# Sums of the second product's weights tied behind the blocks of the first: a hybrid decoder block on one core

## The chip, the cores and the metric

The kernel runs on one core of a Trainium2 chip. The core has five engines that work side by side, each through its own queue, in the order in which the instructions were put there: TensorE (PE in the profile; PEld is its weight load), VectorE (DVE), ScalarE (ACT), GpSimd (POOL) and SyncE (SP). DMAs are issued from the queues of SP and ACT. The metric is the device time of one execution in microseconds (us), lower is better. A profiled execution gives a trace with a start, a duration and, where an engine stood idle, a releaser for each instruction.

## The reference

The program is one decoder layer on a sequence of 1024 rows with 1024 channels: a token-selecting attention and a causal convolution side by side, merged by gates, then a dense feed-forward part, all in float32. The change lies in the feed-forward part:

```python
h = modulate(rmsnorm(x, norm_ffn_g[l]), sh_f, sc_f)
a, b = jnp.split(h @ w_ffn_in[l], 2, axis=-1)              # (1024 x 1024) @ (1024 x 5632)
x = x + g_f[:, None, :] * ((jax.nn.silu(a) * b) @ w_ffn_out[l])   # (1024 x 2816) @ (2816 x 1024)
return rmsnorm(x, norm_final_g)
```

## The kernel before

Both products are done in Strassen-Winograd form: instead of eight products of quarter matrices, seven, with sums and differences of quarters on both sides. Each float32 operand is split into a high part (rounded by ACT, L1190) and a low part (the rest, by VectorE or GpSimd, L1191), and one product of quarters is high x high, high x low and low x high: `prod`, L1211 to L1213, 12 matmuls of 128x512. The splits of the weight side go through eight places of a tile `sa`; the activation side (`h2a`, and `T`, which holds B22 and T1 to T4) is split once (`split_t`, L1336 and L1337).

The first product runs over 22 blocks n, one for each 128 columns of w_ffn_in in both halves. A block loads two pieces of w_ffn_in into the tile `ws` (two buffers, `stage_w`, SP), adds them up on VectorE (`s_sums`, L1241 to L1244), and evacuates its PSUM banks. For the first seven blocks (n < NPRE = 7) the two products on h2a come early (`do_m1`, `do_m2`, L1226, L1233), while T is still being made from the last rows of the normed input, and the five others later (`do_apart`). From block 7 on (`do_sums`) two further products are added into the same bank `u`: this is the steady part. The last instruction of a steady block is L1289, `e0 = u * e0` on VectorE, which also frees the bank of u. After each odd block `g_sums` makes the sums of the activation side of the second product from two blocks and stores seven pieces (L1305, seven DMAs on ACT's queue).

The second product needs sums of the quarters of w_ffn_out as well: T1 to T4. `w_sums(j)`, j = 0 to 10, makes them for one j. It loads two row blocks of w_ffn_out (512 KB each) into two buffers of the tile `wt` (L1312, SP), does four VectorE sums in place (L1315 to L1318), and stores the four results to DRAM (L1320, four DMAs on ACT's queue), from where the second product reads them. The tile wt has two buffers, so the loads of set j+1 wait for the stores of set j. In the program text two sets stand behind each odd block from block 7 on, but the text does not set the order. A scheduler places each instruction on its engine by a simulated timeline; what depends on nothing can be placed far ahead. `after(ins, prev)` ties an instruction behind another in the order only, without a semaphore.

## Time and profile before

| | |
|---|---|
| runs | 1620.33 us median of 3 (1613.86 to 1622.17) |
| profiled execution | 1617.23 us, its span 1615.5 us |
| TensorE busy | 1496.8 us, 93% of the span |
| VectorE busy | 1184.9 us, 73% |
| ScalarE busy | 692.0 us, 43% |
| GpSimd busy | 550.6 us, 34% |
| mean granted TensorE clock | 0.971 |
| the chain that ended last | TensorE 53%, VectorE 27%, DMA 8% |

The shares are means over stages with different limits. The stage of the change begins at 935 us, when TensorE leaves the output projection, and its blocks from number 7 on run from about 1114 us. The granted clock is given as a share of 2.4 GHz.

### The profile page before, as it was taken

The numbers are of one execution on the slowest core, as the hardware profiler recorded it, in microseconds if no ns is written. First come the engines' busy times: TensorE is split into PE (matmuls) and PEld (weight loads), VectorE is DVE, ScalarE is ACT, GpSimd is POOL, SyncE is SP. The second block draws the span as 40 slices with busy tenths as digits, with TensorE's granted clock in tenths as the row PEclk, the third lists the DMA queues.
The fourth block names the chain that finished last, engine by engine and source line by source line (L and its number), as shares of the span: only waits on it lengthen the run. The fifth ranks groups of instructions, "written<-read, shape, count | busy, mean of one in ns | idle before, by whom it ended". The sixth has DMA issues, their size and how long they took to land.

```text
span 1615.5 us, 19899 instructions
## 1 busy us (share of the span) xinstructions
PE 1496.8 (93%) x6880; PEld 1203.3 (74%) x6880; DVE 1184.9 (73%) x2100; ACT 692.0 (43%) x1243; POOL 550.6 (34%) x411
## 2 busy tenths in 40 slices
PE   5998999999769999989989997998999999999996
PEld 3776777787648887768767886776888888888875
DVE  5698768999985657756695589998666666555688
ACT  4301456767135555755333344123333333344344
POOL 0232215798939894101440255320000000004172
PEclk9999999999969999989999998999999999999998
DMA  9335332232212222345763435776333334766682
GB/s 348 111 121 186 122 113 56 62 104 86 80 44 66 59 59 79 99 163 163 249 218 120 143 131 176 248 244 230 124 105 98 98 98 138 241 195 193 196 274 106
DMA packets 193597, 232.15 MB, mean 144 GB/s; under 512 B 12152, under 2 KB 126040, under 8 KB 193496
## 3 DMA queue, kind: packets, MB, share of 16 engines
q1 hardware_dynamic: 164416, 174.39, 34.4%
q10 hardware_dynamic: 29080, 56.48, 9.2%
q8 instruction: 54, 0.88, 0.2%
q14 instruction: 47, 0.39, 0.1%
HBM read 167.12 MB, written 59.51 MB: 140 GB/s over the span
## 4 chain that ended last, share of the span: by engine, by line
PE 53%; DVE 27%; DMA 8%; issue 4%; ACT 3%; POOL 3%; SPq 0%; ACTq 0%; DVEq 0%; POOLq 0%
DVE cy L527 5%; PE pj L326 4%; DVE jk L714 4%; PE pj L327 4%; PE pj L328 4%; PE qk L567 3%; PE qk L1211 3%; PE qk L1212 3%; PE qk L1213 3%; PE qk L1115 2%; PE pj L1211 2%; PE pj L1212 2%; PE pj L1213 2%; PE pj L1115 2%; PE pv L870 1%
## 5 line engine op out<-in xcount | busy, mean ns | idle before, releaser
L326 PE MATMUL pj<-hT,wh 128*128 128x512 f32 (+1 forms) x592 | 242.7, 410 | 15.0 <-DVE z L494 5.5
L327 PE MATMUL pj<-hT,wh 128*128 128x512 f32 (+1 forms) x592 | 234.9, 397 | 0.0
L328 PE MATMUL pj<-hT,wl 128*128 128x512 f32 (+1 forms) x592 | 234.5, 396 | 0.0
L125 POOL TENSOR_TENSOR wl<-ws,wh 128x1024 fp32r<-128x1024 f32 (+2 forms) x49 | 127.0, 2593 | 266.9 <-ACT wh L124 241.4
L1476 POOL TENSOR_TENSOR cb<-cb 128x512 f32<-128x512 f32 x8 | 18.1, 2268 | 395.4 <-DVE cb L1495 395.4
L326 PEld LDWEIGHTS pj<-hT,wh 128*128 128x128 f32 (+1 forms) x592 | 112.8, 191 | 42.5 <-DVE z L494 5.7
L1419 DVE TENSOR_TENSOR sa<-sab,sa 128x1024 fp32r<-128x1024 f32 x66 | 94.5, 1438 | 64.5 <-ACT sa L1418 57.8
L328 PEld LDWEIGHTS pj<-hT,wl 128*128 128x128 f32 (+1 forms) x592 | 112.3, 190 | 26.2 <-issue 0.8
L327 PEld LDWEIGHTS pj<-hT,wh 128*128 128x128 f32 (+1 forms) x592 | 112.8, 191 | 19.5 <-issue 0.6
L1418 ACT ACTIVATE sa<-sab 128x1024 fp32r<-128x1024 f32 x66 | 69.9, 1060 | 101.9 <-PE pt L1425 31.0
L1190 ACT ACTIVATE sa<-s 128x512 fp32r<-128x512 f32 x88 | 55.0, 631 | 127.3 <-DMA tT<-wt 26.0
L714 DVE TENSOR_SCALAR_CACHE_REDUCE jk<-M,F 128x640 f32<-128x640 f32 (+4 forms) x136 | 104.4, 821 | 1.7 <-POOL M L675 0.4
L842 ACT ACTIVATE P<-qk,mins 128x384 f32<-128x384 f32 (+4 forms) x96 | 55.2, 578 | 99.0 <-DVE mins L837 94.6
L527 DVE SCALAR_TENSOR_TENSOR cy<-z,dwc,cy 128x511 f32<-128x511 f32 (+29 forms) x120 | 87.9, 801 | 0.1
L724 ACT ACTIVATE jka<-M,F 128x896 f32<-128x896 f32 x64 | 69.7, 1092 | 34.5 <-DVE F L735 31.9
L857 DVE TENSOR_TENSOR PT<-pt,PT 128x512 fp32r<-128x512 f32 (+1 forms) x80 | 50.6, 634 | 38.8 <-ACT PT L856 38.2
L124 ACT ACTIVATE wh<-ws 128x1024 fp32r<-128x1024 f32 (+2 forms) x51 | 48.3, 948 | 69.1 <-PE pj L327 45.1
L466 POOL TENSOR_TENSOR gy<-gy,pr 128x512 f32<-128x512 f32 (+30 forms) x60 | 76.5, 1274 | 2.0
L466 POOL TENSOR_TENSOR cy<-cy,pr 128x512 f32<-128x512 f32 (+30 forms) x60 | 74.1, 1235 | 4.7
L1211 PE MATMUL qk<-T,sa 128*128 128x512 f32 x176 | 69.7, 397 | 6.4 <-ACT E L1226 6.4
L1190 ACT ACTIVATE sa<-ws 128x512 fp32r<-128x512 f32 x66 | 40.9, 629 | 80.4 <-PE qk L1212 26.8
L1191 DVE TENSOR_TENSOR sa<-s,sa 128x512 fp32r<-128x512 f32 x74 | 54.2, 748 | 23.2 <-ACT sa L1190 23.2
(462 smaller groups left out, 4091.5 us busy)
## 6 DMA issues: line engine op xcount, KB each, us to landing
ws<-in_w_ffn_in SPq DMA_DIRECT2D x51, 512.0 KB, 3.8
ws<-in_w_in SPq DMA_DIRECT2D x40, 512.0 KB, 3.6
mst<-in_w_ada SPq DMA_DIRECT2D x32, 512.0 KB, 3.9
wt<-in_w_ffn_out SPq DMA_DIRECT2D x22, 512.0 KB, 3.5
tT<-wt ACTq DMA_DIRECT2D x44, 256.0 KB, 2.4
sab<-gS SPq DMA_DIRECT2D x44, 256.0 KB
sab<-tT SPq DMA_DIRECT2D x44, 256.0 KB, 3.0
sab<-gA SPq DMA_DIRECT2D x33, 256.0 KB, 3.8
```

The source lines that it names most:

```text
L125: (eng or lo_eng[0]).tensor_tensor(view(lo), view(st), view(hi).bitcast(F32), op=ALU.subtract)
L326: nc.tensor.matmul(p_[:m], wh[:, k, :], hh, start=(k == 0), stop=False)
L327: nc.tensor.matmul(p_[:m], wh[:, k, :], hl, start=False, stop=False)
L328: nc.tensor.matmul(p_[:m], wl[:, k, :], hh, start=False, stop=(k == nk - 1))
L466: g_.tensor_tensor(y[:, a:hi], y[:, a:hi], pr[:, : hi - a], op=ALU.add)
L527: v_.scalar_tensor_tensor(y[:, a:hi], z[:, a - sft : hi - sft], tap(cc, CW - 1 - sft), y[:, a:hi], op0=ALU.mult, op1=ALU.add)
L714: v_.tensor_scalar(jk[:, : (tb + 1) * P], M[tb], thr[:, i : i + 1], 0.0, op0=op, op1=ALU.add, accum_out=cnt[:, i : i + 1])
L1190: s_.activation(d[:, 0, :], src, AF.Copy)
L1211: nc.tensor.matmul(bank, a[:, 0, ks], bh, start=(first and k == 0), stop=False, skip_group_check=True)
L1212: nc.tensor.matmul(bank, a[:, 0, ks], bl, start=False, stop=False, skip_group_check=True)
L1213: nc.tensor.matmul(bank, a[:, 1, ks], bh, start=False, stop=(k == 3), skip_group_check=True)
L1419: eng.tensor_tensor(lo, st, hi.bitcast(F32), op=ALU.subtract)
```

## The change

`do_sums` returns its last instruction (L1289), and `w_sums` ties its first two sums behind that instruction of the block after which it is called. The loads, the other two sums and the stores are as before; these follow from the first two by their data.

```diff
         prod(u, r["A22"], T4, False)
-        v_.tensor_tensor(e0, u, e0, op=ALU.mult)
+        return v_.tensor_tensor(e0, u, e0, op=ALU.mult)
...
-    def w_sums(j):
+    def w_sums(j, prev):
 
         rows_ = []
         for f in (j, j + NH2):
...
         (b11, b12), (b21, b22) = rows_
-        v_.tensor_tensor(b11, b12, b11, op=ALU.subtract)
-        v_.tensor_tensor(b12, b22, b12, op=ALU.subtract)
+        for ins in (v_.tensor_tensor(b11, b12, b11, op=ALU.subtract), v_.tensor_tensor(b12, b22, b12, op=ALU.subtract)):
+            after(ins, prev)
         v_.tensor_tensor(b22, b22, b11, op=ALU.subtract)
         v_.tensor_tensor(b21, b21, b22, op=ALU.subtract)
...
             do_m2(n)
-            do_sums(n)
+            last_e = do_sums(n)
         if n % 2:
             g_sums(n)
             for _ in range(0 if n < NPRE else 2):
                 if todo_w:
-                    w_sums(todo_w.popleft())
+                    w_sums(todo_w.popleft(), last_e)
```

What this does to the order of the instructions is seen at three places. In the rows, a name with its number is one tile; both of the first two sums read L1315 in the new kernel, since they stand in one line.

The first place is VectorE's queue where the last quarter of T is made: h_1590 is the last piece of the normed input, L1158 the end of its preparation, and L1337 with T_8668 the low half of T1. The rows before:

```order
L1243 TENSOR_TENSOR s_1629_8737<-ws_8732,ws_8734 128x512
L1318 TENSOR_TENSOR wt_9598<-wt_9598 128x512
L1356 SCALAR_TENSOR_TENSOR h_1581_8218<-h_1581_8218,h2a 128x512
L1158 TENSOR_TENSOR h_1590_8273<-h_1590_8273,h2a 128x512
L1315 TENSOR_TENSOR wt_9869<-wt_9869 128x512
L1233 TENSOR_TENSOR E_8530<-pv_8545,E_8530 128x512
L1242 TENSOR_TENSOR s_1628_8736<-s_1628_8736,ws_8732 128x512
L1191 TENSOR_TENSOR sa_8294<-s_1628_8736,sa_8294 128x512
L1233 TENSOR_TENSOR E_8566<-qk_8581,E_8566 128x512
L1350 TENSOR_TENSOR h_1590_8273<-h_1590_8273 128x512
L1233 TENSOR_TENSOR E_8602<-pj_8617,E_8602 128x512
L1337 TENSOR_TENSOR T_8668<-h_1590_8273,T_8668 128x4x128
```

And the same place in the new kernel, up to the fourth sum of the block, L1244:

```order
L1356 SCALAR_TENSOR_TENSOR h_1581_8218<-h_1581_8218,h2a 128x512
L1158 TENSOR_TENSOR h_1590_8273<-h_1590_8273,h2a 128x512
L1241 TENSOR_TENSOR s_1628_8736<-ws_8734 128x512
L1243 TENSOR_TENSOR s_1629_8737<-ws_8732,ws_8734 128x512
L1350 TENSOR_TENSOR h_1590_8273<-h_1590_8273 128x512
L1233 TENSOR_TENSOR E_8530<-pv_8545,E_8530 128x512
L1242 TENSOR_TENSOR s_1628_8736<-s_1628_8736,ws_8732 128x512
L1337 TENSOR_TENSOR T_8668<-h_1590_8273,T_8668 128x4x128
L1233 TENSOR_TENSOR E_8566<-qk_8581,E_8566 128x512
L1191 TENSOR_TENSOR sa_8294<-s_1628_8736,sa_8294 128x512
L1244 TENSOR_TENSOR s_1629_8737<-ws_8732,s_1628_8736 128x512
```

The sums on wt are gone from here, L1158 stands ahead of L1241 and L1243, and L1337 on T_8668 stands ahead of two evacuations (L1233) and a split (L1191) that came before it.

The second place is VectorE's queue in steady block 10, in the new kernel: wt_9881 and wt_9883 are the second set behind block 9, L1280 and L1285 evacuate block 10, L1191 on ws_10020 is the split of A22 of block 11, and L1241 begins the sums of block 12:

```order
L1191 TENSOR_TENSOR sa_8294<-s_1748_10023,sa_8294 128x512
L1315 TENSOR_TENSOR wt_9881<-wt_9881 128x512
L1191 TENSOR_TENSOR sa_8294<-ws_10034,sa_8294 128x512
L1280 TENSOR_TENSOR G_9932<-pv_9933,G_9932 128x512
L1285 TENSOR_TENSOR G_9932<-qk_9989,G_9932 128x512
L1315 TENSOR_TENSOR wt_9881<-wt_9883,wt_9881 128x512
L1191 TENSOR_TENSOR sa_8294<-ws_10020,sa_8294 128x512
L1317 TENSOR_TENSOR wt_9883<-wt_9883,wt_9881 128x512
L1287 TENSOR_TENSOR G_9932<-G_9932 128x512
L1318 TENSOR_TENSOR wt_9883<-wt_9883 128x512
L1233 TENSOR_TENSOR E_9974<-qk_10042,E_9974 128x512
L1241 TENSOR_TENSOR s_1761_10182<-ws_10180 128x512
```

Before, the same rows stood there without the four on wt. The two rows that follow are L1243 and then L1289 of block 10; the first set (wt_9869 and wt_9871) stands right behind L1289 of block 9, its L1316 six rows behind it, with other rows between.

The third place is SP's queue, which issues the loads of ws for the blocks (L1196) and those of wt (L1312). The steady part of it before:

```order
L1196 DMA ws_9909<-in_w_ffn_in 128x8x128
L1196 DMA ws_10020<-in_w_ffn_in 128x8x128
L1196 DMA ws_10034<-in_w_ffn_in 128x8x128
L1196 DMA ws_10180<-in_w_ffn_in 128x8x128
L1196 DMA ws_10194<-in_w_ffn_in 128x8x128
```

And in the new kernel:

```order
L1196 DMA ws_9909<-in_w_ffn_in 128x8x128
L1196 DMA ws_10020<-in_w_ffn_in 128x8x128
L1196 DMA ws_10034<-in_w_ffn_in 128x8x128
L1312 DMA wt_9881<-in_w_ffn_out 128x1024
L1312 DMA wt_9883<-in_w_ffn_out 128x1024
L1196 DMA ws_10180<-in_w_ffn_in 128x8x128
L1312 DMA wt_10154<-in_w_ffn_out 128x1024
L1312 DMA wt_10156<-in_w_ffn_out 128x1024
L1196 DMA ws_10194<-in_w_ffn_in 128x8x128
```

Before, all loads of wt stood ahead of the steady part, between the loads of ws for the first blocks; now 20 of the 22 stand between the loads of the steady blocks. The stores (L1320) moved on ACT's queue in the same way.

## Rows read from the trace of the kernel before

**Rows 1.** Windows of the first product: busy us (instructions) per engine, granted clock, DMA.

```profile
core 0: us, PE busy (x) PEld busy (x) DVE busy (x) ACT busy (x) POOL busy (x), PEclk, DMA share, GB/s
935.44:1000.00 64.56, 55.66 (x233) 44.05 (x232) 62.11 (x79) 32.39 (x57) 42.06 (x23) 0.92 0.48 161
1000.00:1098.96 98.96, 92.31 (x392) 73.66 (x390) 92.81 (x127) 23.02 (x38) 24.40 (x15) 0.98 0.74 247
1098.96:1121.00 22.04, 15.65 (x58) 12.65 (x59) 17.83 (x30) 7.54 (x14) 0.00 (x0) 0.85 0.71 244
1121.00:1340.00 219.00, 219.00 (x958) 179.39 (x957) 140.34 (x223) 82.35 (x139) 0.00 (x0) 1.00 0.33 106
```

**Rows 2.** Waits of TensorE from 860 us on: total us, times, longest.

```profile
PE qk L1211 <- ACT E L1226: 6.4, 1, 6.4
...
PE pj L1211 <- ACT T L1336: 3.9, 1, 3.9
PE pj L1211 <- ACT sa L1190: 2.6, 1, 2.6
...
PE pj L1211 <- DVE G L1257: 2.0, 1, 2.0
PE pj L1213 <- POOL sa L1191: 1.2, 2, 0.7
PE pt L1211 <- DVE G L1260: 0.9, 1, 0.9
```

**Rows 3.** Windows of the instructions on tile wt alone: VectorE busy (instructions).

```profile
935.44:985.00 49.56, 10.13 (x9) 0.92 0.44 149
1000.00:1100.00 100.00, 25.89 (x27) 0.98 0.74 248
```

**Rows 4.** Timeline of VectorE, first window: start, duration, instruction, idle before it.

```profile
938.74 1.23 DVE L1316 TENSOR_TENSOR wt<-wt,wt 128x512 f32<-128x512 f32 x1 [2.03 <-DMA wt<-in_w_ffn_out]
...
983.11 0.67 DVE L1337 TENSOR_TENSOR T<-h,T 128x512 fp32r<-128x512 f32 x1
```

**Rows 5.** Timeline of TensorE, its first matmul on T.

```profile
978.62 0.79 PE L1211 MATMUL pt<-T,sa 128*128 128x512 f32 x1 [5.02 <-ACT T L1336]
```

**Rows 6.** Timeline of GpSimd and VectorE over one early block.

```profile
1045.81 1.75 POOL L1191 TENSOR_TENSOR sa<-ws,sa 128x512 fp32r<-128x512 f32 x1
...
1052.82 0.69 DVE L1241 TENSOR_TENSOR s<-ws 128x512 f32<-128x512 f32 x1 [0.53 <-DMA ws<-in_w_ffn_in]
...
1056.66 1.29 POOL L1191 TENSOR_TENSOR sa<-s,sa 128x512 fp32r<-128x512 f32 x1 [9.09 <-ACT sa L1190]
1056.76 1.73 DVE L1315 TENSOR_TENSOR wt<-wt 128x512 f32<-128x512 f32 x1 [0.25 <-issue]
...
1061.49 1.65 POOL L1191 TENSOR_TENSOR sa<-ws,sa 128x512 fp32r<-128x512 f32 x1
```

**Rows 7.** Timeline of VectorE and ScalarE at the last wait of TensorE.

```profile
1103.03 0.69 DVE L1315 TENSOR_TENSOR wt<-wt 128x512 f32<-128x512 f32 x1 [1.51 <-DMA gS<-G]
...
1104.72 0.58 ACT L1226 ACTIVATE E<-qk 128x512 f32<-128x512 f32 x1
```

**Rows 8.** Timeline of VectorE and TensorE in steady block 10.

```profile
1164.59 0.68 DVE L1289 TENSOR_TENSOR E<-pj,E 128x512 f32<-128x512 f32 x1
...
1177.33 0.68 DVE L1191 TENSOR_TENSOR sa<-ws,sa 128x512 fp32r<-128x512 f32 x1
...
1182.73 0.68 DVE L1242 TENSOR_TENSOR s<-s,ws 128x512 f32<-128x512 f32 x1
1183.34 0.68 DVE L1289 TENSOR_TENSOR E<-qk,E 128x512 f32<-128x512 f32 x1
...
1187.50 0.40 PE L1211 MATMUL qk<-h2a,sa 128*128 128x512 f32 x1
```

**Rows 9.** DMAs, issue to landing: stores L1320, then loads L1312, then ws (steady).

```profile
DMA to landing us min/median/max: 2.0/2.4/6.4
...
DMA to landing us min/median/max: 3.3/3.5/3.9
...
ws<-in_w_ffn_in SPq DMA_DIRECT2D x24, 512.0 KB, 3.9
```

## The prediction

> **What bounds the kernel now.** I read the page first (shares of each engine, and the slices in which TensorE's digit falls below 9), then windows over those slices, then who TensorE waited for, and only then single rows. The windows show where TensorE is not fed [rows 1]. From 1121 to 1340 us, the steady part of the first product, it has no idle at all: 958 matmuls in 219 us, 219/957 = 0.229 us each, granted clock 1.00, and VectorE is busy for 140.34 of 219 us, so it has 78 us to spare. In the three windows before it TensorE stands still now and then and the granted clock is 0.92, 0.98 and 0.85. With 0.229 us for each matmul (and about 0.9 us for eight short transposes in the first) their work would take 224 x 0.229 + 0.9 = 52.2, 391 x 0.229 = 89.5 and 58 x 0.229 = 13.3 us. They take 64.56, 98.96 and 22.04 us, which is 12.4, 9.5 and 8.7 us more: **30.6 us lost in all**. The eight waits of TensorE are 5.0 and 3.9 us in the first window, 2.0, 2.6, twice 0.6 and 0.9 in the second and 6.4 in the third, 22.0 us together [rows 2, 5]; I put the other 8.6 us down to matmuls at a lower granted clock beside these waits.
>
> In the same windows VectorE is full: 62.11 of 64.56, 92.81 of 98.96, 17.83 of 22.04 us [rows 1]. Its instructions on the staging tile wt, which are the sums that the change moves, take 10.13 us (9 of them) up to 985 us, and 25.89 us (27) between 1000 and 1100 us [rows 3].
>
> **The change, part by part.** Nothing is added or taken out: 44 VectorE sums, 22 loads on SP, 44 stores on ACT. All but the first sum lay in these windows; all now stand behind block 7 or a later odd block, two sets (eight sums) behind each. So VectorE, ACT's queue and SP's queue lose work in the windows that lose time, and get it back in the steady part.
>
> *First window, 12.4 us lost.* TensorE stood from 978.62 - 5.02 = 973.6 [rows 5]. To go on at full pace it needs both halves of the last quarter of T1; the low half comes from VectorE's L1337 at 983.11, done at 983.78 [rows 4]. Ahead of that, from 938.74 on, VectorE spent 10.0 us on eight of the nine moved sums (the ninth has only just begun at 985) and 2.03 us waiting for wt [rows 3, 4]. Without them the low half is there at 983.8 - 12.0 = 971.8; the new order also puts three other instructions behind it (two evacuations and a split), 0.6 us each, which gives 970.0. Against this: some of the moved sums took about 1.7 us where others take 0.68, as the sum at 1056.76 (1.73 us), which falls into GpSimd's split at 1056.66 [rows 6]. If such a collision passes to the next VectorE instruction, four of them cost 4 x 1.05 = 4.2 us again, and the low half comes at 974.2. So TensorE waits 0 to 0.6 us for it in place of 8.9. The second product needs S4's low half from GpSimd, two VectorE instructions, an ACT copy and a GpSimd split later, so I leave 2 us of loss in this window (bounds 0 and 5).
>
> The Trainium skill, page "SBUF — State Buffer", section "Who interferes with whom", says that a VectorE instruction with two SBUF inputs and a GpSimd instruction that reads SBUF take one read interface by turns, the later one blocked for the whole instruction. By that rule a wait belongs to whichever instruction comes next, so 974.2 holds and not 970.0, and the relief in this window is 4.2 us of VectorE time smaller. The 1.73 us beside 0.68 agrees with it.
>
> *Second window, 9.5 us lost.* Here the loop from one block's load to the next is longer than TensorE's block of 60 matmuls, 60 x 0.229 = 13.7 us. GpSimd ends its last split at 1045.81 + 1.75 = 1047.56, which frees ws; the load lets L1241 start at 1052.82; GpSimd ends the next block's last split at 1061.49 + 1.65 = 1063.14 [rows 6]. That is 15.6 us. The sum at 1056.76 stands between L1241 and L1244 and goes (1.73 us): 13.9. The load took 5.3 us while wt loads and stores were under way; in the steady part its median is 3.9 us [rows 9], which gives 12.5. So the loop lies between 13.9 and 12.5, at TensorE's pace or below. The stores of g_sums remain on ACT's queue, and the first block that reuses their tile still waits for them. I leave 3 us of the 9.5 (bounds 0 and 8).
>
> *Third window, 8.7 us lost.* This is one wait: VectorE's L1315 at 1103.03 waited 1.51 us, ACT's store of it stood ahead of L1226, which came at 1104.72, and TensorE had waited 6.4 us for that evacuation [rows 2, 7]. In the new order no store of wt stands there. I leave 1 us (bounds 0 and 4).
>
> *Steady part.* The cover is VectorE's 78 us, of which 44 x 0.69 = 30 us are taken. But the sums also wait there. After L1289 of block 9 (1164.59) the first set's L1316 is the sixth further row on, so it ends near 1168.9, rows being 0.61 us apart [rows 8]; its store lands 2.4 us later and the next load 3.5 us after that [rows 9], at 1174.8. VectorE comes to the second set's first sum at about 1172.4 and so stands for 2.4 us. Its second sum waits in the same way for the last store of the first set and stands some 0.7 us. Queued behind it is the split of A22 (L1191, 1177.33 in the trace [rows 8]), which comes 1.3 us later; the load of the next b half waits for that split, and L1241 and L1289 wait for the load: L1289 of block 10 comes 0.8 us later than its 1183.34. It frees the bank that the matmul at 1187.50 writes [rows 8], so there are 1187.50 - 1184.02 = 3.5 us to spare, and 2.7 remain. Block 11 has no sums and recovers. SP's loads of ws behind the wt loads are late by the same 1.3 us. I take 1 us for this. The bounds are 0, and 8: if store and load both take their longest, 6.4 and 3.9 us [rows 9], L1289 comes 5.2 us late, TensorE waits 1.7 us in each of five pairs.
>
> **Sum.** 30.6 - 2 - 3 - 1 - 1 = 23.6 us gained. The profiled execution took 1617.23 us (span 1615.5), 3.1 us below the median of the three runs, 1620.33, which lie between 1613.86 and 1622.17. From the profiled execution the new time is 1593.6; from the median 1596.7. I take **1594 us**.
>
> **Rivals.**
> (a) *All of it comes back*, every bound at its good end: 1617.2 - 30.6 = 1587 us. For it: all eight waits lie where VectorE is full. Against it: the collisions with GpSimd and the g_sums stores stay. Chance 0.2.
> (b) *Another limit takes over in the middle window and the first*: the block loop stays at 13.9 us or more because the load keeps its 5.3 us, and the T quarters come late through GpSimd. All bad ends there: 5 + 8 + 4 = 17 of the 30.6 stay, with 1 in the steady part the gain is 12.6: 1605 us. For it: ACT and GpSimd wait on one another in this stage as well. Chance 0.2.
> (c) *Slower: VectorE stands on the wt loads in the steady part and TensorE's bank comes late.* The place is L1289 behind the second set. It costs nothing until store and load are 2.7 us longer than the 5.9 us taken above, and each further us costs 1 us in each of five pairs, plus the lower granted clock. To undo the gain of 23.6 us takes 4.7 us a pair, that is store and load together at 13.3 us; the longest seen together are 10.3. Slower than before by 0.5%, 1628 us, needs 14.9. Chance 0.04.
> (d) *Nothing is gained*, because another producer ends at the same moment as the moved sums: 1617 us. Against it: in the third window the chain runs through the moved sum itself. Chance 0.06.
> The forecast itself has 0.5.
>
> **How the numbers follow.** 1594 is the likeliest case. Its own range is 1589 to 1600. The 80% range is 1586 to 1607: it takes in (a) and (b), leaving out (c), (d) and the tails. A change of 0.5%, 8 us, is about what a measurement of this kernel can tell from none. Forecast, (a) and most of (b) are faster by more: 0.87. Within 0.5%: the rest of (b) and (d), 0.09. Slower: 0.04.
>
> **What would show it.** In the profile after: no instruction on wt between 935 and 1114 us; TensorE's waits for L1336, L1226 and L1257 gone or under 2 us, with a granted clock near 1.00 from 935 us on; the first-product stage then shorter by 20 us or more; in the steady part VectorE busy some 0.14 more, with waits of 2 to 3 us ahead of the second set's L1315 and none on TensorE. Waits of TensorE for L1289, L1275 or a ws load in the blocks behind odd ones would be rival (c). TensorE waits of more than 10 us in all that remain ahead of 1100 us would be (b). The prediction is wrong if the steady part loses more than 10 us or the first three windows keep more than half of their 30.6.

## The result and the profile after

The changed kernel takes 1604.89 us (median of 5 runs, 1600.88 to 1606.38) against 1615.62 us for the kernel before (median of 5, 1613.86 to 1622.17): ratio 0.9917, 95% interval 0.9904 to 0.9931. The profiled execution took 1604.89 us, its span 1603.0, which is 12.5 us below the span before. The forecast was 1594, a gain of 23.6 us; the medians differ by 10.7 and the profiled executions by 12.3. (The median before was 1620.33 over the three runs known when the forecast was made, and is 1615.62 over five.)

To see where the time went, I cut both traces at five marks of TensorE's own work: the last matmul on wo (L1115), the third product of block 1 (bank pt), the first matmul for block 7 (on h2a), the first for block 8, and the first matmul of the second product (L1423). The matmuls between two marks are the same in both kernels.

| us between the marks | before | after | without loss |
|---|---|---|---|
| wo to block 1 (first window) | 69.0 | 64.5 | 57.0 |
| block 1 to block 7 (second) | 86.2 | 83.5 | 76.2 |
| block 7 to block 8 (third) | 20.1 | 12.3 | 11.1 |
| block 8 to the second product (steady) | 272.3 | 272.8 | 272.3 |

The last column: the second and third row are those of a kernel below (`four_ws`), in which TensorE never waits there; the first is 64.5 less the 7.5 us that the start of two products shows to be lost (below); the last is the kernel before. So the loss was 12.0 + 10.0 + 9.0 = 31.0 us and is now 7.5 + 7.3 + 1.2 = 16.0. The stage gained 15.0, the steady part gave back 0.6. TensorE left wo 1.9 us later in this execution (such differences are spoken of under four_ws), and the rest of the program took 0.1 longer: 15.0 - 0.6 - 1.9 - 0.1 = 12.4, but for rounding the 12.5 us by which the spans differ.

The windows of the kernel after between these marks, which answer to [rows 1], with the same steady window of 219 us; the columns are the same:

```profile
937.13:1001.59 64.46, 60.44 (x253) 48.37 (x251) 55.59 (x74) 33.45 (x59) 35.39 (x23) 0.95 0.25 74
1001.59:1085.09 83.50, 78.54 (x338) 64.00 (x336) 68.72 (x92) 20.79 (x35) 22.06 (x15) 0.98 0.39 124
1085.09:1097.34 12.25, 11.36 (x50) 8.94 (x49) 9.90 (x17) 3.53 (x6) 0.00 (x0) 1.00 0.44 147
1121.00:1340.00 219.00, 218.96 (x954) 178.66 (x953) 157.19 (x255) 79.20 (x138) 0.00 (x0) 1.00 0.61 201
```

VectorE, which filled these windows before, now has 9 us free in the first and 15 in the second, and the DMA share has halved. The granted clock is still 0.95 and 0.98 in them. Who TensorE waited for from 860 us on, which answers to [rows 2] (total, times, longest):

```profile
PE pj L1211 <- DVE G L1260: 3.6, 2, 2.9
PE pt L1212 <- DVE T L1337: 3.4, 1, 3.4
PE pj L1424 <- DVE sa L1419: 2.9, 1, 2.9
...
PE pt L1211 <- ACT sa L1190: 1.3, 1, 1.3
PE qk L1211 <- ACT E L1226: 0.9, 1, 0.9
PE pt L1213 <- DVE sa L1191: 0.6, 1, 0.6
```

The waits for L1336 and L1257 are gone, and the 6.4 us for L1226 are 0.9. In their place stand L1337 in the first window and L1260 in the second. The waits of the stage are 9.8 us, from 22.0; L1424 belongs to the second product, where 2.3 us were waited before too.

**First window.** VectorE's and TensorE's timelines, which answer to [rows 4, 5]:

```profile
941.90 0.69 DVE L1233 TENSOR_TENSOR eg<-qk,eg 128x512 f32<-128x512 f32 x1 [3.27 <-ACT eg L1226]
...
977.13 1.75 DVE L1337 TENSOR_TENSOR T<-h,T 128x512 fp32r<-128x512 f32 x1
978.80 0.68 DVE L1233 TENSOR_TENSOR E<-qk,E 128x512 f32<-128x512 f32 x1
979.40 0.67 DVE L1191 TENSOR_TENSOR sa<-s,sa 128x512 fp32r<-128x512 f32 x1
```

The first of these rows in the kernel before, where it follows the sums and waits for nothing:

```profile
943.30 0.68 DVE L1233 TENSOR_TENSOR eg<-qk,eg 128x512 f32<-128x512 f32 x1
```

```profile
975.10 0.40 PE L1211 MATMUL pt<-T,sa 128*128 128x512 f32 x1
978.93 0.61 PE L1212 MATMUL pt<-T,sa 128*128 128x512 f32 x1 [3.43 <-DVE T L1337]
980.13 0.79 PE L1213 MATMUL pt<-T,sa 128*128 128x512 f32 x1 [0.59 <-DVE sa L1191]
980.73 0.63 PE L1211 MATMUL pt<-T,sa 128*128 128x512 f32 x1
981.15 0.63 PE L1212 MATMUL pt<-T,sa 128*128 128x512 f32 x1
```

The low half of T1 is done at 978.88, or 976.96 on the clock of the kernel before (1.92 us less): 6.8 us earlier than its 983.78, not 9.6 to 13.8. TensorE waits for it and then for block 0's S1. Behind these 4.0 us of waiting its matmuls come 0.43 us apart, not 0.23: the granted clock from 978.9 to 985 is 0.52, close to the 1.2 GHz level. The product that starts at 975.10 takes until 984.57, 9.47 us in place of 2.72, and the next one 3.42: 7.5 us lost, of which 4.0 are waits.

**Second window.** The loop from one block's split of A22 (L1191 on GpSimd, which frees ws) to the next block's, which answers to [rows 6]:

```profile
1039.19 1.29 POOL L1191 TENSOR_TENSOR sa<-ws,sa 128x512 fp32r<-128x512 f32 x1 [1.74 <-ACT sa L1190]
```

```profile
1044.27 0.69 DVE L1241 TENSOR_TENSOR s<-ws 128x512 f32<-128x512 f32 x1 [4.34 <-DMA ws<-in_w_ffn_in]
```

```profile
1054.58 0.63 ACT L1190 ACTIVATE sa<-ws 128x512 fp32r<-128x512 f32 x1 [4.23 <-DVE E L1302]
```

```profile
1055.29 1.29 POOL L1191 TENSOR_TENSOR sa<-ws,sa 128x512 fp32r<-128x512 f32 x1 [2.94 <-ACT sa L1190]
...
1070.71 1.29 POOL L1191 TENSOR_TENSOR sa<-ws,sa 128x512 fp32r<-128x512 f32 x1 [1.74 <-ACT sa L1190]
```

```profile
1075.63 0.69 DVE L1241 TENSOR_TENSOR s<-ws 128x512 f32<-128x512 f32 x1 [2.48 <-DMA ws<-in_w_ffn_in]
...
1079.84 0.68 DVE L1260 TENSOR_TENSOR G<-pj,G 128x512 f32<-128x512 f32 x1
```

```profile
1080.67 0.47 PE L1211 MATMUL pj<-T,sa 128*128 128x512 f32 x1 [2.93 <-DVE G L1260]
```

From 1039.19 to 1055.29 are 16.1 us, to 1070.71 another 15.4. Over the five turns of this part the mean is 15.3, where TensorE needs 13.6 to 13.7. VectorE now stands before each L1241 for the load of ws, and the evacuation L1260, which sits behind L1241 in its queue, frees TensorE's bank late. In the longer turn ACT's copy of A22 stood 4.2 us behind stores of g_sums, which waited for VectorE's L1302. In the turn after it the copy at 1070.00 was released by TensorE, as it was in the turn that the prediction read in the kernel before, at 1060.78:

```profile
1070.00 0.63 ACT L1190 ACTIVATE sa<-ws 128x512 fp32r<-128x512 f32 x1 [3.22 <-PE qk L1213]
```

```profile
1060.78 0.63 ACT L1190 ACTIVATE sa<-ws 128x512 fp32r<-128x512 f32 x1 [1.02 <-PE pv L1213]
```

**Steady part.** The first sum now stands at 1114.7 and the last at 1314.5. What VectorE waited for in front of instructions on wt there:

```profile
  DMA wt<-in_w_ffn_out: 10.9, 4
  issue: 8.1, 2
```

That is 19 us, 3.8 for each of the five pairs of sets, and no wait of TensorE came of it. (For the two under "issue" the profile names no releaser; they stand at the same row as the others and are as long, 4.1 and 3.9 us.)

### The profile page after: what moved, and what is told of

It is laid out like the page before. It is cut to its first block, busy times and chain, and to the rows that moved or that the text cites. A ratio compares the mean times of both kernels' runs of the same rounds, so it can differ in the third digit from the quotient of the medians.

```text
span 1603.0 us, 19901 instructions
## 1 busy us (share of the span) xinstructions
PE 1495.4 (93%) x6880; PEld 1203.2 (75%) x6880; DVE 1176.6 (73%) x2100; ACT 689.7 (43%) x1243; POOL 539.4 (34%) x411
## 5 line engine op out<-in xcount | busy, mean ns | idle before, releaser
L1419 DVE TENSOR_TENSOR sa<-sab,sa 128x1024 fp32r<-128x1024 f32 x66 | 94.5, 1438 | 64.5 <-ACT sa L1418 60.7
L1190 ACT ACTIVATE sa<-s 128x512 fp32r<-128x512 f32 x88 | 54.3, 629 | 116.8 <-DVE s L1242 47.4
L1190 ACT ACTIVATE sa<-ws 128x512 fp32r<-128x512 f32 x66 | 40.7, 627 | 86.6 <-DMA ws<-in_w_ffn_in 25.7
L1211 PE MATMUL qk<-T,sa 128*128 128x512 f32 x176 | 68.7, 390 | 0.9 <-ACT E L1226 0.9
L1212 PE MATMUL qk<-T,sa 128*128 128x512 f32 x176 | 68.6, 390 | 0.0
```

The costliest lines, as they stand in the source:

```text
L1190: s_.activation(d[:, 0, :], src, AF.Copy)
L1211: nc.tensor.matmul(bank, a[:, 0, ks], bh, start=(first and k == 0), stop=False, skip_group_check=True)
L1212: nc.tensor.matmul(bank, a[:, 0, ks], bl, start=False, stop=False, skip_group_check=True)
L1419: eng.tensor_tensor(lo, st, hi.bitcast(F32), op=ALU.subtract)
```

## The experiments

The windows in this table are of the profiled executions, between the same marks. The device time is the median, and the ratio is to the kernel before as it ran beside each (medians of 1615.6 to 1618.7 us). A kernel that ran once has no interval.

| kernel | first | second | third | steady | device time, ratio to before |
|---|---|---|---|---|---|
| before | 69.0 | 86.2 | 20.1 | 272.3 | 1615.6 |
| after | 64.5 | 83.5 | 12.3 | 272.8 | 1604.9, 0.9917 (0.9904 to 0.9931) |
| no_sums | 64.5 | 86.5 | 12.0 | 272.3 | 1605.1, 0.9919 (0.9906 to 0.9932) |
| four_ws | 64.3 | 76.2 | 11.1 | 273.3 | 1593.4, 0.9847 (0.9831 to 0.9863) |
| t1_first | 64.5 | 83.5 | 12.3 | 273.1 | 1604.6, 0.9908 (0.9892 to 0.9923) |
| both | 63.5 | 76.2 | 11.1 | 274.5 | 1592.8, 0.9843 (0.9828 to 0.9858) |
| s4_first | 66.5 | 76.2 | 11.1 | 274.7 | 1594.2, 0.9850 (0.9834 to 0.9866) |
| copy_first | 64.5 | 80.3 | 13.8 | 274.7 | 1602.1, 0.9902 (0.9881 to 0.9924) |
| first_set_free | 65.9 | 81.3 | 15.0 | 273.6 | 1610.0 (one run) |
| old_no_stores | 71.8 | 89.0 | no wait | | 1614.2 (one run) |
| old_stores_only | 63.9 | 84.7 | 13.1 | 272.3 | 1614.0 (one run) |
| three_sets | 64.5 | 83.6 | 12.3 | 289.9 | 1619.0 (one run) |
| three_sets_pool | 64.0 | 84.0 | 12.5 | 284.8 | 1617.9 (one run) |
| three_sets_loads | 64.5 | 84.1 | 12.3 | 297.8 | 1629.6 (one run) |

In old_no_stores TensorE takes the products in another order around two of the marks. The first is worked out from the product behind it (bank pv), and for the third window only the starts of its products are read: they follow one another without a wait. Its steady part has no such mark to start from.

**Does what is left come from the sums at all?** no_sums, on the changed kernel:

```diff
-            for _ in range(0 if n < NPRE else 2):
-                if todo_w:
-                    w_sums(todo_w.popleft(), last_e)
...
         if opb[0] == "T":
-            src = tb_d[opb][j]
+            f, h = {"T1": (j, 0), "T3": (j, 1), "T2": (j + NH2, 1), "T4": (j + NH2, 0)}[opb]
+            src = w_ffn_out[f * P : (f + 1) * P, hs(h)]
```

> The changed kernel without the moved work: the 22 loads of wt, the 44 sums and the 44 stores are left out, and the second product reads raw quarters of w_ffn_out (same size, same number of loads) in place of T1 to T4. Theory: what the change did not bring back (15.6 us of the 30.6 still lost between the last w_o matmul and block 11) has nothing to do with the sums any more, and in the steady part they cost 0.5 us. Then the time is that of the changed kernel less 0 to 1.5 us (about 1604), with the same waits of TensorE for L1337 (3.4 us) and L1260 (2.9 us). Rival: the sums still cost in their new place, through the DMA share (0.61 against 0.33 before) or at the start of the second product: then at least 4 us less, 1601 or below.

Measured: 1605.1 us, the changed kernel's time. The first window is the same to 0.1 us, and the steady part 0.5 shorter. So the 44 sums, 22 loads and 44 stores cost 0.5 us in their new place in these two executions (the other kernels below that keep two sets there have a steady part of 273.1 to 274.7 us, 0.8 to 2.4 over the kernel before), and the 16 us still lost in the stage are not theirs. One miss: the long wait of the second window stood before the same product but for ACT's copy (L1190, 5.2 us), not for L1260 (2.9); the second window lies between 81.3 and 86.5 us in kernels in which nothing of it was changed.

**What is the second window's limit?** four_ws, on the changed kernel:

```diff
-        a21, a22 = r["b"] = stage_w(DFF + order[n] * P)
+        a21, a22 = r["b"] = stage_w(DFF + order[n] * P, "wl" if n < NPRE and n % 2 else "ws")
...
-            r["a"] = stage_w(order[n] * P)
+            r["a"] = stage_w(order[n] * P, "wl" if n < NPRE and n % 2 else "ws")
```

> The changed kernel with the blocks 1, 3 and 5 of the do_apart part staging both weight halves under the tag wl, which nothing else uses in that stretch, so that there are four staging tiles in place of two. Theory: the middle window loses 7.2 us (1.6 at 1045 to 1052, 0.9 at 1063, 4.8 at 1080) because the next block's load waits for the split of A22, VectorE stands 2 to 5 us for it at L1241, and the bank evacuation L1260 queues behind that. With four tiles the load is there a block ahead: VectorE's idle time ahead of L1241 (20.7 us in 8 waits) falls under 5 us, TensorE's waits for L1260 go, and 6 to 7 us come back: about 1598. Rival: the pace is set by the ring of sa tiles, by GpSimd, or by the g_sums stores that stand ahead of the A22 copy on ACT: then the waits only move (to L1190 or L1191), under 3 us come back, 1602 or more.

Measured: 1593.4 us, and the second and third windows lose nothing. TensorE's waits from 936 to 1121 us are all in the first window:

```profile
PE pt L1212 <- DVE T L1337: 3.4, 1, 3.4
PE pt L1213 <- DVE sa L1191: 0.4, 1, 0.4
```

VectorE's idle time before L1241 fell from 18.6 us in 6 waits to 2.6 in 2 (985 to 1085 us), as the theory had it:

```profile
DVE s L1241 <- DMA ws<-in_w_ffn_in: 2.6, 2, 1.5
```

The mean turn from one split of A22 to the next fell from 15.3 to 12.4 us (991.08 to 1052.98, five turns). So the second window's limit was the loop through the two buffers of ws: shown. The second and third window give 8.5 us; the median fell by 11.5, more than the 6 to 7 us that I expected. This execution also left wo 3.6 us earlier than that of the changed kernel: it came to the first matmul on wo 1.7 us earlier, and has no wait at L1141, where the changed kernel waited 1.9 us for VectorE's L1131. The mark lies between 932.4 and 940.1 us in the kernels here (946.0 in old_stores_only, which has 14 of its 22 loads and 26 of its 44 stores ahead of it); why it moves was not followed up.

**Which part of that loop?** copy_first, on the changed kernel: in the first blocks `g_sums(n - 1)` is written behind block n's splits, and its stores are tied behind the copy of A22.

```diff
-            nc.scalar.dma_start(ga_d[op][j], t)
+            st = nc.scalar.dma_start(ga_d[op][j], t)
+            if copy:
+                after(st, copy)
...
+            if n and n % 2 == 0:
+                g_sums(n - 1, last_copy[0])
```

> The changed kernel with two staging tiles, where in the do_apart part the g_sums of an odd block are written behind the next block's splits, and their seven stores are tied on ACT's queue behind that block's copy of A22. With four tiles the middle window's 7.2 us all came back; this asks which part of the loop made it too long. In the changed kernel the loop took 16.1 us in the blocks with g_sums stores and 14.2 to 15.4 us in the others; the copy of A22 at 1054.58 stood 4.2 us behind stores that waited for VectorE. Theory: without these stores ahead of it the copy comes 2.2 us earlier or more, the loop falls to 13.5 to 14.5 us, and 3 to 6 of the 7.2 us come back: 1599 to 1602. Rival 1: the load of ws (3.6 to 5.2 us) and the ring of sa tiles set it: less than 2 us, 1603 or more. Rival 2: the tiles E and G come free later, and TensorE waits for an evacuation into a new G (L1257): no gain, or a loss.

Measured: the edit missed its target. The copy that stands behind the stores of g_sums is not that of the next block but that of the block after it, since the splits run further ahead than I had taken them to; so the tie moved nothing there. ACT's timeline in this kernel (line numbers one higher) still has the stores first:

```profile
1050.05 0.33 ACTq L1306 DMA_DIRECT2D gA<-E  x1
1050.65 0.33 ACTq L1306 DMA_DIRECT2D gA<-G  x1
1051.25 0.33 ACTq L1306 DMA_DIRECT2D gS<-E  x1
1051.70 0.63 ACT L1191 ACTIVATE sa<-ws 128x512 fp32r<-128x512 f32 x1 [4.24 <-DVE E L1303]
```

The turns with these stores stayed at 16.2 and 17.0 us (16.0 and 16.1 in the changed kernel), but the three others fell from 14.8, 14.2 and 15.4 to 13.3, 13.1 and 14.3. In no other kernel with the new order and two buffers is the first of them under 14.6 or the second under 14.2, so the edit did shorten these; why was not followed up. The second window lost 4.1 us in place of 7.3 and the third 2.8 in place of 1.2; both windows differ by as much between other kernels here, and the interval holds the changed kernel's ratio. What the stores ahead of the copy cost stays open; that the turn goes through the two buffers of ws is what four_ws shows.

**Is the first window a matter of VectorE's order?** t1_first, on the changed kernel, and both, which adds the four staging tiles:

```diff
+    for i in range(4):
+        split_t(T1, h2b[i][:, 0:4, :], slice(i * P, (i + 1) * P), v_)
+    st_[0].pop("a")
+    split_in(0, "S1")
+    s1_low = last_lo[0]
...
-        split_t(T1, u, ts_, v_)
...
+            after(t, s1_low)
```

> The changed kernel with VectorE's order in the conversion stage turned round: the four splits of T1 and block 0's S1 are written ahead of the rest, and the sums for T4 are tied behind the low half of S1. Theory: TensorE waits 3.4 us for the last quarter of T1 and 0.6 for S1, and runs at the lower clock behind that, 7.5 us in all, because these two stand behind T4's six instructions on VectorE. Now the low half of T1 ends near 969 and that of S1 between 973 and 976, where TensorE is ready at 975.1: the wait falls to 0 to 1 us. What then happens behind it is open. If the ring of sa tiles starts the block loop earlier along with TensorE, 5 to 7 us stay: 1598 to 1600. If the loop, 15.4 us a block against TensorE's 13.7, keeps its own times, the middle window takes it back: less than 2 us, 1603 to 1605, with longer waits for L1260. A rival: T4 is now late itself, a wait of 3 us or more for T4 at the fifth product: no gain.

> Four staging tiles and the turned order together. Theory: the two places hold 7.2 and 7.5 us of the 15.6 that are still lost, and with both taken away 12 to 14 us come back: 1591 to 1593, ratio to the kernel before about 0.985. If one of them only hides the other, the sum is no more than the better of the two alone, 1598.

Measured: t1_first 1604.6 us, both 1592.8, no better than without the new order within the intervals. The wait for T1 is gone, and others stand in its place. TensorE's waits in both, 970 to 990 us (its line numbers are one higher, so L1191 is the high half, L1192 the low half, L1227 the evacuation):

```profile
975.01 0.50 PE L1212 MATMUL pv<-T,sa 128*128 128x512 f32 x1 [1.71 <-ACT sa L1191]
976.68 0.79 PE L1214 MATMUL pv<-T,sa 128*128 128x512 f32 x1 [0.93 <-POOL sa L1192]
981.77 0.80 PE L1212 MATMUL pj<-T,sa 128*128 128x512 f32 x1 [0.45 <-ACT E L1227]
```

These are the second product's S4 (high half from ACT, low half from GpSimd), and then a bank that ACT has to evacuate. With the lower clock behind them 6.5 us are lost, where four_ws lost 7.3. None of the cases that I had written down is right: T4 was not late, and the loop took nothing back; the first window itself kept the loss. The time expected for both, 1591 to 1593, came by luck: four_ws alone brought it. The last try moved S4's sum ahead of T4's as well. s4_first, on both:

```diff
             after(t, s1_low)
+            after(t, last_s4[0])
```

> Four staging tiles and the turned order, with the sums for T4 tied behind the sum for S4 as well. With the turned order TensorE no longer waited for T1, but 1.7 us for ACT's copy of S4, 0.9 for GpSimd's low half of it and 0.5 for ACT's L1227, and lost 6.5 us at this place, where the order before lost 7.3. Theory: S4's sum ran at 973.6 though its operands were there at 967.3, behind four sums for T4; now it comes 4 to 5 us earlier, the waits for S4 go, and 2 to 4 us come back: 1589 to 1591. Rival: T4's sums free the h tiles into which the evacuation L1227 writes, and one more product has to wait for that: the wait only moves on, and the time stays within 1.5 us of 1592.8.

Measured: 1594.2 us. All the waiting of the stage is now in one place, as the rival had it (L1228 is the evacuation L1226 of the changed kernel):

```profile
PE pj L1213 <- ACT E L1228: 6.2, 1, 6.2
```

```profile
983.90 0.60 ACT L1228 ACTIVATE E<-pj 128x512 f32<-128x512 f32 x1 [2.90 <-POOL T L1339]
```

The first window, 66.5 us, is longer than in any other order tried. The second row tells why the evacuation came late: it was released by GpSimd's split for T4 (L1339, T<-h, 979.28 to 983.87), which reads an h tile; E and the h tiles share the same seven buffers (tag f4). That is the rival's mechanism. The split took 4.59 us beside six VectorE instructions of 128x512 without a gap, where the next two of its kind took 1.26 and 1.28. So the first window has three limits within a few us of each other: T1 and S1, then S4, then ACT's evacuation into a tile E.

**Did the sums at the head of the stage cost anything?** first_set_free, on the changed kernel:

```diff
-            after(ins, prev)
+            if j:
+                after(ins, prev)
```

> The changed kernel with the first set of sums (four of the 44) left untied, so that it stands where it stood before: one sum ahead of the last w_o block, three at the head of the conversion stage, behind L1128 and ahead of the first block's L1233; the other ten sets stay behind the steady blocks. My prediction took the 2.0 us of waiting and 4.6 us of sums there off VectorE's path to the last quarter of T1. New theory: in the changed kernel VectorE stands 3.3 us at that very place for the first block's evacuation by ACT, so that these sums filled a wait and gave back 3.3 us at most. Then putting them back delays the first L1233 by 3 to 3.5 us and the last low half of T1 (14.2 us ahead of TensorE's wait end) by 0 to 3.5 us; TensorE's wait for T1 goes from 3.4 to between 3.4 and 7 us. By the prediction's own count it would go up by the full 6.6 us, to 10.

VectorE's timeline at that place (the set's last three sums, which read L1315, L1318 and L1319 in this kernel):

```profile
943.53 1.33 DVE L1315 TENSOR_TENSOR wt<-wt,wt 128x512 f32<-128x512 f32 x1 [1.93 <-DMA wt<-in_w_ffn_out]
944.97 1.60 DVE L1318 TENSOR_TENSOR wt<-wt,wt 128x512 f32<-128x512 f32 x1
946.61 1.66 DVE L1319 TENSOR_TENSOR wt<-wt 128x512 f32<-128x512 f32 x1
948.19 0.68 DVE L1233 TENSOR_TENSOR eg<-qk,eg 128x512 f32<-128x512 f32 x1
```

Measured from the end of L1128: L1233 starts after 6.6 us here (941.60 to 948.19) and after 3.3 in the changed kernel, which waits there for ACT. The low half of T1 ends after 41.5 us here and after 40.3 there. So 6.6 us of sums and waiting cost 3.3 us at L1233 and 1.3 at T1. TensorE waits 3.2 us for T1, no more than before, behind a new 1.2 us for L1148 further ahead; the first window is 1.4 us longer. The theory holds for VectorE (3 to 3.5 us at L1233, 0 to 3.5 at T1); the wait, which was to grow from 3.4 to as much as 7, did not. The prediction's count, the full 6.6 us, does not hold. The 1610.0 us of this one run are not all of this place: it left wo 3.0 us later, and its third window is 2.7 us longer.

**VectorE's time, or the stores?** Two halves of the work taken out of the kernel before. old_no_stores leaves out the 44 stores, old_stores_only the 44 sums:

```diff
-        for op, t in (("T1", b11), ("T3", b12), ("T2", b22), ("T4", b21)):
-            nc.scalar.dma_start(tb_d[op][j], t)
```

```diff
-        v_.tensor_tensor(b11, b12, b11, op=ALU.subtract)
-        v_.tensor_tensor(b12, b22, b12, op=ALU.subtract)
-        v_.tensor_tensor(b22, b22, b11, op=ALU.subtract)
-        v_.tensor_tensor(b21, b21, b22, op=ALU.subtract)
```

> The kernel before without the 44 stores of the sums; loads and sums stay at their old places, and the second product reads raw quarters of w_ffn_out. This tells VectorE's time apart from the stores on ACT's queue and their DMA traffic. TensorE lost, worked out group by group, 11.8 us at the first quarter of T1, 10.0 us in the middle window and 9.0 us behind the last do_apart block before the change, and 7.5, 7.2 and 1.1 after it. Theory: the last one is ACT's store ahead of L1226, so without stores at most 2 us of its 9.0 are left; the first is VectorE's time, so 10 to 12 us stay; in the middle the store traffic and VectorE share it, 5 to 10 us. Rival: VectorE's time counts alone: all three stay within 1.5 us of the kernel before.

> The counterpart: the kernel before without the 44 sums; the 22 loads and the 44 stores stay, the stores now wait for the loads alone, and what is stored is the raw quarters. Theory: the first place, VectorE's time, goes to the 7.5 us of the changed kernel; the middle keeps 7 to 10 us, since the block loop runs through the load of ws, which shares the DMA with wt loads and stores; in the last place no store waits for a sum, so under 3 us of the 9.0 are left. Rival, the stores hold ACT wherever they stand: 5 us or more stay in the last place too.

Measured, as losses in the three windows: before 12.0, 10.0, 9.0; without stores 14.8, 12.8, none; without sums 6.9, 8.5, 2.0. The first window goes by VectorE's sums: without them it stands at about the changed kernel's loss, without the stores it is not better (14.8 where 10 to 12 was expected). One reserve: old_stores_only left wo 10.8 us later, with 14 loads and 26 stores already issued, so its window does not start from the same state, and its whole time is hardly lower. The third goes by the store that waits for a sum ahead of L1226: either half taken out ends the long wait. The second keeps its loss in both, so neither half alone set it, and no_sums, without sums, loads and stores, loses 10.3 us there; that it gets worse without stores is a second miss (5 to 10 expected). TensorE's waits without sums, 946 to 1121 us, show the old waits for L1336 gone, 1.7 us left of the 6.4 for L1226, and the second window's still there (L1333 is the low half of T in this kernel):

```profile
PE pj L1211 <- ACT sa L1190: 5.2, 1, 5.2
PE pt L1213 <- DVE sa L1191: 1.8, 1, 1.8
PE qk L1211 <- ACT E L1226: 1.7, 1, 1.7
...
PE pt L1212 <- DVE T L1333: 1.0, 1, 1.0
```

**How far is the steady part from rival (c)?** three_sets, on the changed kernel, then with the stores, and then instead with the loads, on GpSimd's queue:

```diff
-            for _ in range(0 if n < NPRE else 2):
+            for _ in range(0 if n < NPRE else 3):
```

```diff
-            nc.scalar.dma_start(tb_d[op][j], t)
+            nc.gpsimd.dma_start(tb_d[op][j], t)
```

```diff
-            nc.sync.dma_start(st.rearrange("p a b -> p (a b)"), w_ffn_out[f * P : (f + 1) * P, :])
+            nc.gpsimd.dma_start(st.rearrange("p a b -> p (a b)"), w_ffn_out[f * P : (f + 1) * P, :])
```

> The changed kernel with three sets behind an odd steady block in place of two (blocks 7, 9 and 11 take three, 13 takes two). The prediction had the second set cost TensorE nothing because L1289 of the next block has 3.5 us to spare and comes 0.8 us late. A third set needs one more round of store and load (2.4 + 3.5 us) less the rows between, and four more sums (2.4 us): VectorE stands another 2 to 3 us and L1289 comes 4 to 6 us later than without sums. Theory: TensorE waits 1 to 3 us for L1289's bank behind blocks 7, 9 and 11, 3 to 9 us with the lower clock: the steady part grows from 0.5 us over the kernel before to 4 to 10 us. If VectorE catches up elsewhere, as with two sets, the steady part stays within 1 us.

> Three sets behind an odd steady block as before, with the 44 stores of the sums issued from GpSimd, which has nothing else to do there, in place of ACT. With the stores on ACT the steady part lost 17 us, all in waits for ACT's L1275 and L1279, not for L1289. Theory: those evacuations stood behind stores on ACT that waited for a sum, which waited for a load. With the stores elsewhere the waits for L1275 go and the steady part loses under 3 us, though VectorE still stands for the third set's loads. Rival: VectorE itself is what is late, and L1275 waits because VectorE's split or sum ahead of it is: then 10 us or more stay, in other waits.

> Three sets behind an odd steady block, stores on ACT again, and the 22 loads of wt issued from GpSimd in place of SP. Moving the stores off ACT did not help (14 us still lost in the steady part), so ACT's queue is not what is late first. New theory: SP's queue. A wt load waits there for the store of the set before it to land (73 us in 25 waits), and the next block's ws load stands behind it: it was issued at 1148.0 where the changed kernel has it at 1138 to 1145, VectorE stood 5.3 us for it at L1241, and ACT's copy of S2, with L1275 behind it, came late. With the wt loads on another queue the ws loads are issued in time and the steady part loses under 4 us. Rival: VectorE is late because its own sums wait for wt (17.6 us in 8 waits): then 10 us or more stay, behind waits of VectorE for wt.

Measured: the steady part is 17.1, 12.0 and 25.0 us longer than with two sets, more than expected, and the waits are for ACT's evacuation L1275, not for L1289. TensorE's waits from 1121 to 1340 us in three_sets, then those of VectorE in three_sets:

```profile
PE qk L1211 <- ACT G L1275: 7.2, 2, 3.6
PE pj L1211 <- ACT G L1275: 4.0, 2, 2.3
PE pj L1211 <- ACT G L1279: 0.6, 1, 0.6
```

```profile
DVE s L1241 <- DMA ws<-in_w_ffn_in: 27.6, 11, 5.3
DVE wt L1315 <- DMA wt<-in_w_ffn_out: 17.6, 8, 4.1
```

VectorE's waits for wt are 17.6 us here, 23.7 in three_sets_pool and 31.8 in three_sets_loads. Freeing ACT's queue of the stores did not end the loss, and freeing SP's of the loads made it worse, so my two theories fall. The rival of the last kernel, VectorE late because it stands for wt, agrees with the 10 us and more that stayed, but it is not shown: from three_sets to three_sets_pool these waits rise (17.6 to 23.7) while the loss falls (17.1 to 12.0). The move to GpSimd also changed the way of the loads (4.5 us from issue to landing there, 4.3 in the changed kernel), so that test is not a clean one; which queue is late first stays open. With two sets the steady part is already near this limit: in four_ws, t1_first, both, s4_first, copy_first and first_set_free TensorE has one or two waits of 0.4 to 1.0 us there, all for L1275.

## Why the prediction was right in direction and too high in size

- **What bounds the kernel:** right. Losses of 31.0 us by the marks, 30.6 in the prediction, in the three windows named.
- **Third window:** right. 1 us was to stay, 1.2 stayed. old_no_stores and old_stores_only, one run each, show the mechanism: the store behind a waiting sum held L1226.
- **Steady part:** right. 1 us was to be lost; 0.6 measured, 0.5 by no_sums (0.8 to 2.4 in the other kernels with two sets). VectorE stood 3.8 us for each pair of sets, 3.1 were worked out; the loads of wt took 4.3 us from issue to landing there, not the 3.5 of [rows 9]. VectorE's busy share there rose by 0.08, not 0.14: the same 219 us now hold other blocks than before.
- **First window:** the failed step. 2 us were to stay (0 to 5), 7.5 stayed. "Ahead of that, from 938.74 on, VectorE spent 10.0 us on eight of the nine moved sums (the ninth has only just begun at 985) and 2.03 us waiting for wt [rows 3, 4]. Without them the low half is there at 983.8 - 12.0 = 971.8". The first 6.6 us of these filled a wait: without them VectorE stands 3.3 us for ACT's L1226, so half comes back. From L1233 to the low half of T1, 7.0 us should have gone (five sums at 5.2 us, three moved instructions at 0.6); 40.48 became 36.98, so 3.5 went.
  - The other 3.5 passed on to instructions that ran beside GpSimd, for which the prediction had allowed 4.2: in this stretch L1131 took 1.70 us after and 0.75 before, one L111 1.22 after and 0.16 before, the last L1337 1.75 and 0.67. Outside the moved sums 10 VectorE instructions of 128x512 took over 0.9 us before, 11 after, and each of the 11 lay beside a GpSimd split for at least 1.2 us. The Trainium skill's page "SBUF — State Buffer", section "Who interferes with whom", says that a VectorE instruction with two SBUF inputs and a GpSimd instruction that reads SBUF exclude one another. The trace agrees for these 11, though no run here takes GpSimd's splits away.
  - Together this puts T1 at 977.0 on the old clock, 2.8 us past the bad end of 974.2: in the main the 3.3 us for ACT, which the prediction had nowhere, less the 0.7 by which the collisions stayed under their allowance.
  - A wait costs more than its length: 4.0 us of waiting cost 7.5, since the granted clock was 0.52, near its lower level, for some 6 us behind it. In t1_first, both and s4_first T1 came in time, and 6.5 us or more were still lost in this window, to S4 and to ACT's evacuation.
- **Second window:** the size failed within its bounds. 3 us were to stay (0 to 8), 7.3 stayed. "So the loop lies between 13.9 and 12.5, at TensorE's pace or below": it is 15.3. The sum between L1241 and L1244 did go, and five of the six loads that VectorE waited for took 3.6 to 4.0 us (the sixth 5.2, with no wt traffic beside it). But the sum's 1.73 us did not come off: from L1241 to the block's last split on GpSimd were 8.7 us before (1052.82 to 1061.49) and are 8.9 to 11.0 now. That split needs ACT's copy of A22, and the copy was released by TensorE already before the change (1060.78 above), so the sum was not what this turn waited for last. The one turn that I had read (15.6 us) is also one of the shorter: five turns before (997.9 to 1081.5) have a mean of 16.7. Five turns take 15.3 each in no_sums, without any of the moved work, and 15.0 in old_stores_only, without the sums.
- **The sum:** 30.6 - 2 - 3 - 1 - 1 = 23.6 was to be gained; by the marks 15.0 - 0.6 = 14.4 was. Rival (b), 1605 us, is nearest: another limit took over in the second window and the first. It had 0.2, the forecast 0.5. That its time is met so closely is luck. The block loop stayed long, but not because the load kept its 5.3 us, and T1 came late on VectorE, not through GpSimd; what stayed is 7.5, 7.3 and 1.2 us, not 5, 8 and 4. The waits left are 9.8 us, just under its mark of 10. The prediction's own test for being wrong, more than half of the loss kept in the windows, is met by a hair: 16.0 of 31.0. The range held the time, though the first window's term lay outside its own bounds (7.5 against 5).

## What to carry to other kernels

Before counting an instruction's time as gained, look at what its engine would do in that time: sums in front of a wait are free as far as the wait reaches, and taking them out shows the wait (3.3 of 6.6 us here). Work a loop's length out over several turns, follow in each what its last step was released by, and ask what is in it that the change leaves alone; here the limit of the middle blocks was two staging buffers, and giving them the buffers that the change had left idle there (four_ws) brought another 0.7%. Where several producers end within a few us of each other, taking the latest away moves the wait to the next one.

## What the runs showed of the hardware that was not expected

- A wait of TensorE cost up to nearly twice its length: 4.0 us of waiting at 975 us were followed by matmuls 0.43 us apart (granted clock 0.52 from 978.9 to 985.0 us), 7.5 us in all. At 1080.67 a wait of 2.93 us was followed by a granted clock of 0.61 up to 1085, 4.8 us in all. The wait of 1.32 us at 1049.31 was followed by a granted clock of 1.00 up to 1056.
- Loads of wt issued from GpSimd landed 4.5 us after issue, those from SP 4.3, but a GpSimd issue took 0.53 us of its engine and one from SP 0.33.
